# A common sum joins its last product in the PSUM bank: the down projection of a two-layer streaming encoder

## The chip, the cores and the metric

The kernel runs on one core of a Trainium2 chip. The metric is device time in microseconds (us) of one execution; smaller is better. TensorE does the matrix products, VectorE (DVE), ScalarE (ACT) and GpSimd (POOL) the element work, and SyncE (SP) issues most transfers.

## The reference

Two layers of a transformer encoder with D_MODEL = 1024 are computed for 1152 tokens (1024 of a prompt and 8 x 16 of running streams). Each layer does attention, then a SwiGLU feed-forward with D_FF = 2816:

```python
def swiglu(h, w_in, w_out):
    gate, up = jnp.split(h @ w_in, 2, axis=-1)
    return (jax.nn.silu(gate) * up) @ w_out

for layer in range(DEPTH):
    ...
    xp = xp + swiglu(rmsnorm(xp, norm_ffn[layer]), w_ffn_in[layer], w_ffn_out[layer])
    xs = xs + swiglu(rmsnorm(xs, norm_ffn[layer]), w_ffn_in[layer], w_ffn_out[layer])
y_prompt = rmsnorm(xp, norm_final)
```

The change touches the last product of this, `(...) @ w_out` added to x: the down projection, once in each layer. All in float32.

## The kernel before

**Numbers in two parts.** A float32 operand is split into a rounded part (`hi`, by ACT, L284) and the rest (`lo`, by `split2`, L285, on POOL or DVE). A product is three matmuls, hi by hi, hi by lo and lo by hi (`passes`, L191 to L193), into one PSUM bank. All have 128 rows and 288 columns (`QW`).

**The down projection** (`down`, called once per layer) adds W_out times the hidden values to x. Of the 22 blocks of 128 hidden rows four are done plainly: two ahead (`firsts`) and two at the end (`finals`), by `step`, L1271. The other 18 are nine pairs in three groups of three pairs (`GROUPS`), and each pair is a Strassen-Winograd scheme of seven products on half-size blocks, in the order b11, t1, t2, t3, t4, b21, b22 (`ORDER`). The sums on the side of the hidden values come from DRAM (`hds`), those on the weights' side are made here (`prep_a`). `product` runs one of the seven for one of 8 output tiles (4 values of j by 2 of q): 3 pairs by 3 matmuls into one bank, then DVE adds the bank to x or to the common sum (L1331). With x seen as four blocks, x11 = `xq(q, j)`, x12 = `xq(2 + q, j)`, x21 = `xq(q, j + 4)`, x22 = `xq(2 + q, j + 4)`: b11 goes to x11 and to the common sum u (`us`, 8 tiles), t1 to x12 and x22, t2 to u, t3 (P7 in the title of the change) to x21 and x22, t4 to x21, b21 to x11, b22 to x12.

**The common sum.** u is complete when t2 of the last group has been added. It belongs to x12, x21 and x22. `combine` (L1334) adds it to them on POOL (L1335), three adds for each of the 8 (j, q), 24 in a layer; they are merged into the work of t3, t4 and b21 of the last group.

**What sets the order.** `merge` deals the preparation of a product (`prep_b`: load and split three pages of hidden sums, POOL; `prep_a`: weight sums and splits, POOL, but for b22 on DVE) between the tiles of the product before. A scheduler then orders the instructions of each engine by its own simulated times; each engine runs its list strictly in that order. PSUM banks come from `ps_any`, which takes the tags m, s, t, s in turn, with 2, 3 and 2 banks. A tile with tag s therefore needs the bank of the tile six before it, and that bank's DVE add done.

**Names in the rows.** `ps` is a bank, `wh` and `wr` weights or their parts, `sd` the weight sum of a pair, `wd` raw weights, `pg` a page (hidden values, their parts, or u), `x` the result, `hd` and `hds` the hidden values in DRAM.

Of the kernel before, what the change touches and what calls it, by code (L numbers as in the profile page):

```python
# [15 lines left out]
ALU = mybir.AluOpType  # L16
# [5 lines left out]
KT = D // P  # L22
# [25 lines left out]
GROUPS = ((1, 2, 3), (4, 5, 6), (7, 8, 9))  # L48
DOWN = ("b11", "t1", "t2", "t3", "t4", "b21", "b22")
ORDER = DOWN  # L50
# [10 lines left out]
def model(ctx: ExitStack, tc: tile.TileContext, I, O):  # L61
    nc = tc.nc
    V, A, G, S, E = nc.vector, nc.scalar, nc.gpsimd, nc.sync, nc.tensor
# [4 lines left out]
    def sb(name, side="left"):  # L68
        return tc.tile_pool(name=name, bufs=1, side=side, reuse_waits="tile")
# [10 lines left out]
    ident = cons.tile([P, P], F32, name="ident")  # L80
# [106 lines left out]
    def passes(out, wts, acts, first=True, last=True, seen=False):  # L187

        n = len(wts)
        for i, ((wh_, wl_), (xh_, xl_)) in enumerate(zip(wts, acts)):  # L190
            E.matmul(out, wh_, xh_, start=first and i == 0, stop=False, skip_group_check=seen)  # L191
            E.matmul(out, wh_, xl_, start=False, stop=False, skip_group_check=seen)  # L192
            E.matmul(out, wl_, xh_, start=False, stop=last and i == n - 1, skip_group_check=seen)  # L193
# [358 lines left out]
    stores, finals = [], []  # L552
# [45 lines left out]
    def merge(*lists):  # L598

        tot = [max(sum(c for c, _ in l), 1) for l in lists]  # L600
        pos, done, out = [0] * len(lists), [0.0] * len(lists), []
        while any(p < len(l) for p, l in zip(pos, lists)):
            i = min((i for i, l in enumerate(lists) if pos[i] < len(l)),
                    key=lambda i: (done[i] + lists[i][pos[i]][0] / 2) / tot[i])
            out.append(lists[i][pos[i]])
            done[i] += out[-1][0]
            pos[i] += 1
        return out
# [342 lines left out]
    def xq(q, k):  # L951

        return X[q // 2][k // 2][:, k % 2, q % 2 * QW:(q % 2 + 1) * QW]
# [14 lines left out]
    def page(n, shape=(4, QW), dt=F32R):  # L968
        return pages[(n >= 8) + (n >= 12) + (n >= 18)].tile([P, *shape], dt, name=nm("pg"), tag=f"g{n}", bufs=1)
# [275 lines left out]
    def down(layer, name, last):  # L1245

        wb = ExitStack()
        pb = wb.enter_context(sb(name + "wb"))
        src = I["w_ffn_out"][layer]
        hrs, bp, ap = [0], [0], [0]  # L1250

        def staged(src, shape):
            t = page(8 + hrs[0] % 4, shape, F32)
            hrs[0] += 1
            S.dma_start(t, src)
            return t


        def prep(f, ops, eng):
            w = weights(src[2 * PLAIN[f // 2] + f % 2], (KT, P), None, eng)  # L1260
            raw = staged(hd[f], (T,))
            hi, lo = (page(f % 2 + n, (T,)) for n in (0, 2))
            split2(hi, lo, raw, eng)
            ops.append((w, (hi, lo)))

        def step(ops, q, j, hook=None):
            o = ps_any()
            c0 = q * QW
            passes(o[:, :QW], [(w[0][:, j, :], w[1][:, j, :]) for w, _ in ops],
                   [(h[0][:, c0:c0 + QW], h[1][:, c0:c0 + QW]) for _, h in ops])  # L1270
            V.tensor_tensor(xq(q, j), xq(q, j), o[:, :QW], ALU.add)  # L1271
            if hook is not None:
                hook(q, j)


        us = [page(4 + q, (4, QW), F32) for q in range(2)]

        def group_load(st, r):

            for k, p in enumerate(st["pairs"]):  # L1280
                st["w", r, k] = t = pb.tile([P, D], F32, name=nm("wd"), tag="wd", bufs=9)
                S.dma_start(t, src[2 * p + r])

        def prep_a(st, n, k):
            f, f1 = st["w", 0, k], st["w", 1, k]
            a11, a12, a21, a22 = f[:, :512], f1[:, :512], f[:, 512:], f1[:, 512:]
            if n == "t1":
                st["s", k] = pb.tile([P, 512], F32, name=nm("sd"), tag="sd", bufs=3)
            z = st.get(("s", k))
            if n == "t1":  # L1290
                G.tensor_tensor(z, a21, a22, ALU.add)
            elif n == "t2":
                V.tensor_tensor(z, z, a11, ALU.subtract)
            elif n == "t3":
                G.tensor_tensor(a11, a11, a21, ALU.subtract)
            elif n == "b22":
                V.tensor_tensor(z, a12, z, ALU.subtract)
            raw = {"b11": a11, "t3": a11, "t4": a22, "b21": a12}.get(n, z)
            i = ap[0] % 3
            if i == 0:  # L1300
                ap[1:] = [wp.tile([P, 2, 4 * VW], F32R, name=nm("wh"), tag="wh", bufs=3)]
            if i < 2:
                hi, lo = (ap[1][:, z, 512 * i:512 * (i + 1)] for z in range(2))
            else:
                t = wp.tile([P, 4 * VW], F32R, name=nm("wr"), tag="wr", bufs=3)
                hi, lo = t[:, :512], t[:, 512:1024]
            ap[0] += 1
            split2(hi, lo, raw, G if n != "b22" else V)
            st[n, "a", k] = hi, lo

        def prep_b(st, n, k):
            raw = staged(hds[st["pairs"][k], DOWN.index(n)], (HALF,))
            t = page((6, 7, 12, 13, 14, 15, 16, 17)[bp[0] % 8], (2, HALF))
            bp[0] += 1
            split2(t[:, 0], t[:, 1], raw, G)
            st[n, "b", k] = t

        def product(st, n, j, q):
            o = ps_any()[:, :QW]
            c = slice(q * QW, (q + 1) * QW)  # L1320
            ks = range(len(st["pairs"]))
            passes(o, [tuple(z[:, j * P:(j + 1) * P] for z in st[n, "a", k]) for k in ks],
                   [(st[n, "b", k][:, 0, c], st[n, "b", k][:, 1, c]) for k in ks])
            u = us[q][:, j]
            x11, x12, x21, x22 = xq(q, j), xq(2 + q, j), xq(q, j + 4), xq(2 + q, j + 4)
            for z in {"b11": (x11, u), "t1": (x12, x22), "t2": (u,), "t3": (x21, x22), "t4": (x21,),
                      "b21": (x11,), "b22": (x12,)}[n]:
                if n == "b11" and z is u and st["first"]:
                    A.copy(u, o)
                else:  # L1330
                    V.tensor_tensor(z, z, o, ALU.add)  # L1331

        def combine(j, q):
            for z in (xq(2 + q, j), xq(q, j + 4), xq(2 + q, j + 4)):  # L1334
                G.tensor_tensor(z, z, us[q][:, j], ALU.add)  # L1335

        firsts, finals = [], []
        run([(1, lambda f=f: prep(f, firsts, V)) for f in range(2)])
        run(x_load(lambda h, i: xd[h, :, 2 * i:2 * i + 2]))
        work, preps = [], []  # L1340
        for i, g in enumerate(GROUPS):
            st = {"pairs": g, "first": i == 0}
            for n in ORDER:
                l = [(1, lambda st=st, r=r: group_load(st, r)) for r in range(2)] if n == ORDER[0] else []
                for k in range(len(g)):
                    l.append((1, lambda st=st, n=n, k=k: prep_b(st, n, k)))
                    l.append((1, lambda st=st, n=n, k=k: prep_a(st, n, k)))
                preps.append(l)
                w = [(1, lambda st=st, n=n, j=j, q=q: product(st, n, j, q)) for j in range(4) for q in range(2)]
                if i == len(GROUPS) - 1 and n in ORDER[3:6]:  # L1350
                    z = ORDER.index(n) - 3
                    w = merge(w, [(1, lambda j=j, q=q: combine(j, q)) for j, q in
                                  [(j, q) for j in range(4) for q in range(2)][3 * z:3 * z + 3]])
                work.append(w)
        preps.append([(1, lambda f=f: prep(f, finals, V)) for f in (2, 3)])
        run(merge([(1, lambda q=q, j=j: step(firsts, q, j)) for q in range(4) for j in range(KT)], preps[0]))
        for w, l in zip(work, preps[1:]):
            run(merge(w, l))
        wb.close()
        pgs[2].close()  # L1360
        pgs[1].close()
        last(lambda q, hook: [(1100, lambda j=j: step(finals, q, j, hook)) for j in range(KT)])
        pgs[0].close()

    def block_tail(li, o_scr, w_src, last, beside=None):
# [126 lines left out]
    with sb("px0", "right") as px:  # L1492
        table(AF.Abs_reciprocal_sqrt)
        first, pre, post = [], [], []
        for ci, (c0, c1) in enumerate(FIRST):
# [7 lines left out]
            st = {}  # L1503
# [73 lines left out]
    with sb("pin1", "right") as pin:  # L1577
        first = [proj_k(I["w_kc"], act, pin, O["c_kt"], kh["c"], kl["c"], ksm["c"], lambda: ps_any("sts")),
                 proj_vt(I["w_vc"], act, pin, O["c_vt"], vs["c"], vsm["c"])]
# [184 lines left out]
```

## Time and profile before

| | |
|---|---|
| median of 3 runs | 2807.08 us (2805.0 to 2810.45) |
| the profiled execution, its own time | 2804.28 us |
| its span (first to last instruction) | 2802.5 us |
| PE busy | 2633.9 us, 94% of the span |
| DVE busy | 1694.0 us, 60% |
| POOL busy | 1247.3 us, 45% |
| ACT busy | 1141.5 us, 41% |
| mean granted TensorE clock, share of full speed | 0.966 |

Busy time is an average over stages with different limits, so the stage in question has to be read by itself. The down projection's groups and finals run from about 1327 to 1560 us in layer 0 and to about 2758 us in layer 1. A row of the timeline has the start, the length (both us), the engine, the line, the operation, output and inputs, the number of instructions merged into the row, and in brackets how long the engine was idle before and who ended that.

### The profile page before, as it was taken

Reading aid. Unit: us, or ns where it says so; the run is one execution under the profiler, and the core shown is the slowest. Engines: PE = TensorE matmul, PEld = TensorE weight load, DVE = VectorE, ACT = ScalarE, POOL = GpSimd, SP = SyncE. Lnnn points to the kernel's source line nnn. Section 1 sums busy time; section 2 is a strip of 40 time slices with the busy share of each in tenths; the row PEclk is TensorE's granted clock in tenths of the full one; section 3 lists DMA queues with packets and bytes.
Section 4 is the critical chain, followed back from the end, with each engine's and each line's share of the span. In section 5 each row is a group of like instructions: output and inputs, shape, how many; then the busy total and the mean of one; then the engine's idle time right before and its main releaser. Section 6 shows DMA issues by size and latency. Waiting matters only on the chain.

```text
span 2802.5 us, 52586 instructions
## 1 busy us (share of the span) xinstructions
PE 2633.9 (94%) x19742; PEld 2522.2 (90%) x19742; DVE 1694.0 (60%) x3583; ACT 1141.5 (41%) x2510; POOL 1247.3 (45%) x1152
## 2 busy tenths in 40 slices
PE   8999988998989999999998998879799999999987
PEld 7999966777989999999998998869799999999987
DVE  7110266766686565566677766855955556556677
ACT  5221366776342222323332566754422222224323
POOL 4212132233443444444996432233434444349993
PEclk8999998999999999999998999989899999999998
DMA  5546587885213232337432132332123223264322
GB/s 159 168 140 205 175 231 227 265 270 179 70 61 103 80 101 86 102 96 244 128 114 90 65 110 81 102 112 64 70 73 98 93 95 99 93 213 165 120 65 91
DMA packets 209840, 357.63 MB, mean 128 GB/s; under 512 B 27817, under 2 KB 134449, under 8 KB 207537
## 3 DMA queue, kind: packets, MB, share of 16 engines
q1 hardware_dynamic: 204976, 349.55, 40.1%
q10 hardware_dynamic: 4608, 4.72, 0.5%
q8 instruction: 155, 2.54, 0.4%
q14 instruction: 101, 0.82, 0.1%
HBM read 252.22 MB, written 101.95 MB: 126 GB/s over the span
## 4 chain that ended last, share of the span: by engine, by line
PE 68%; DVE 10%; DMA 8%; POOL 6%; issue 5%; ACT 2%; SPq 1%; DVEq 0%; ACTq 0%; POOLq 0%
PE ps L191 18%; PE ps L192 18%; PE ps L193 17%; POOL pg L285 2%; PE ps L544 2%; POOL wh L285 2%; PE ps L507 2%; DMA oraw<-od 1%; DVE hf L281 1%; PE ps L505 1%; PE ps L574 1%; DVE pg L285 1%; PE ps L397 1%; PE ps L398 1%; PE ps L396 1%
## 5 line engine op out<-in xcount | busy, mean ns | idle before, releaser
L191 PE MATMUL ps<-pg,wh 128*128 128x288 f32 x3200 | 952.2, 299 | 46.0 <-DVE x L1331 27.0
L192 PE MATMUL ps<-pg,wh 128*128 128x288 f32 x3200 | 952.3, 298 | 3.3 <-POOL pg L285 2.5
L193 PE MATMUL ps<-pg,wh 128*128 128x288 f32 x3200 | 937.4, 296 | 0.6 <-DVE wh L285 0.6
L191 PEld LDWEIGHTS ps<-pg,wh 128*128 128x128 f32 x3200 | 606.5, 190 | 51.4 <-DVE x L1331 27.5
L192 PEld LDWEIGHTS ps<-pg,wh 128*128 128x128 f32 x3200 | 608.5, 190 | 4.8 <-POOL pg L285 3.1
L193 PEld LDWEIGHTS ps<-pg,wh 128*128 128x128 f32 x3200 | 604.3, 190 | 1.2 <-DVE wh L285 0.8
L285 POOL TENSOR_TENSOR wh<-wr,wh 128x1024 fp32r<-128x1024 f32 (+1 forms) x96 | 232.6, 2426 | 349.6 <-ACT wh L284 340.0
L284 ACT CAST wh<-wr 128x1024 fp32r<-128x1024 f32 (+2 forms) x156 | 161.1, 1036 | 248.0 <-PE ps L193 217.9
L192 PE MATMUL ps<-hl,wh 128*128 128x288 f32 x832 | 248.2, 300 | 2.5 <-DVE hl L285 2.3
L191 PE MATMUL ps<-hh,wh 128*128 128x288 f32 x832 | 246.5, 302 | 4.2 <-ACT hh L284 3.1
L193 PE MATMUL ps<-hh,wh 128*128 128x288 f32 x832 | 245.5, 297 | 0.0
L285 POOL TENSOR_TENSOR pg<-pg,pg 128x576 fp32r<-128x576 f32 x126 | 194.8, 1560 | 26.2 <-ACT pg L284 26.2
L1331 DVE TENSOR_TENSOR x<-x,ps 128x288 f32<-128x288 f32 x384 | 156.5, 447 | 81.3 <-PE ps L193 81.1
L284 ACT CAST pg<-pg 128x576 fp32r<-128x576 f32 (+1 forms) x134 | 90.9, 702 | 270.6 <-PE ps L193 145.6
L285 POOL TENSOR_TENSOR wh<-x,wh 128x1024 fp32r<-128x1024 f32 x42 | 101.0, 2406 | 151.2 <-ACT wh L284 151.2
L191 PEld LDWEIGHTS ps<-hh,wh 128*128 128x128 f32 x832 | 156.9, 191 | 8.2 <-ACT hh L284 5.0
L192 PEld LDWEIGHTS ps<-hl,wh 128*128 128x128 f32 x832 | 158.8, 191 | 4.6 <-DVE hl L285 3.4
L193 PEld LDWEIGHTS ps<-hh,wh 128*128 128x128 f32 x832 | 158.6, 191 | 0.1
L285 POOL TENSOR_TENSOR x<-wr,x 128x512 fp32r<-128x512 f32 x44 | 58.5, 1330 | 213.3 <-ACT x L284 208.5
L1191 DVE TENSOR_TENSOR u<-p,ps 128x288 f32<-128x288 f32 x176 | 78.9, 448 | 111.9 <-PE ps L193 111.7
L549 DVE TENSOR_TENSOR pl<-ps,ph 128x512 fp32r<-128x512 f32 (+1 forms) x152 | 92.3, 611 | 34.5 <-ACT ph L548 33.9
L191 PE MATMUL ps<-x,wh 128*128 128x288 f32 x352 | 105.4, 299 | 5.7 <-DVE x L1195 5.7
(296 smaller groups left out, 6202.9 us busy)
## 6 DMA issues: line engine op xcount, KB each, us to landing
wr<-w_ffn_in SPq DMA_DIRECT2D x88, 512.0 KB
hds<-hd SPq DMA_DIRECT2D x252, 144.0 KB
pg<-hds SPq DMA_DIRECT2D x126, 288.0 KB
wd<-w_ffn_out SPq DMA_DIRECT2D x36, 512.0 KB
wr<-w_out SPq DMA_DIRECT2D x22, 512.0 KB
xd<-x SPq DMA_DIRECT2D x16, 576.0 KB
x<-xd SPq DMA_DIRECT2D x16, 576.0 KB
svt<-cache_a_v SPq DMA_DIRECT2D x8, 1024.0 KB
```

Of the source, the lines that this page charges most:

```text
L191: E.matmul(out, wh_, xh_, start=first and i == 0, stop=False, skip_group_check=seen)
L192: E.matmul(out, wh_, xl_, start=False, stop=False, skip_group_check=seen)
L193: E.matmul(out, wl_, xh_, start=False, stop=last and i == n - 1, skip_group_check=seen)
L281: V.scalar_tensor_tensor(out, src, gains[:, gi, k:k + 1], rs, ALU.mult, ALU.mult)
L284: A.copy(hi, src)
L285: eng.tensor_tensor(lo, src, hi, ALU.subtract)
L396: E.matmul(o[:, :width], xh_[:, k], wts[k][0], start=k == 0, stop=False)
L507: E.matmul(sp[:, :w], q2[:, qt], kl2[:, k0:k0 + w], start=False, stop=not dg)
L544: E.transpose(pt[:, col:col + P], tl[:, (kb - kb0) * P:(kb - kb0 + 1) * P], ident)
L549: V.tensor_tensor(fl, pt[:, lo_:hi_], fh, ALU.subtract)
L1191: V.tensor_tensor(st[n, q], st["p1", q], st["x", q][:, :QW], ALU.add)
L1331: V.tensor_tensor(z, z, o, ALU.add)
```

## The change

In the last group, product t3 does not close its bank after its nine matmuls: a tenth one, with the identity as the weights and u as the moving operand, in plain float32, adds u in the bank (L1328). DVE's adds of the bank to x21 and x22 then carry u along. `combine` keeps only the add to x12, 8 in a layer, and moves from the last group's products to the first quarter (q = 0) of the plain block `finals`, behind each of its 8 steps.

```diff
             ks = range(len(st["pairs"]))
+            u = us[q][:, j]
+            fold = n == "t3" and st["last"]
             passes(o, [tuple(z[:, j * P:(j + 1) * P] for z in st[n, "a", k]) for k in ks],
-                   [(st[n, "b", k][:, 0, c], st[n, "b", k][:, 1, c]) for k in ks])
-            u = us[q][:, j]
+                   [(st[n, "b", k][:, 0, c], st[n, "b", k][:, 1, c]) for k in ks], True, not fold)
+            if fold:
+
+                E.matmul(o, ident, u, start=False, stop=True)
...
         def combine(j, q):
-            for z in (xq(2 + q, j), xq(q, j + 4), xq(2 + q, j + 4)):
-                G.tensor_tensor(z, z, us[q][:, j], ALU.add)
+
+            z = xq(2 + q, j)
+            G.tensor_tensor(z, z, us[q][:, j], ALU.add)
...
-                if i == len(GROUPS) - 1 and n in ORDER[3:6]:
-                    z = ORDER.index(n) - 3
-                    w = merge(w, [(1, lambda j=j, q=q: combine(j, q)) for j, q in
-                                  [(j, q) for j in range(4) for q in range(2)][3 * z:3 * z + 3]])
...
-        last(lambda q, hook: [(1100, lambda j=j: step(finals, q, j, hook)) for j in range(KT)])
+
+        def final(q, j, hook):
+            step(finals, q, j, hook)
+            if q == 0:
+                combine(j % 4, j // 4)
+
+        last(lambda q, hook: [(1100, lambda j=j: final(q, j, hook)) for j in range(KT)])
```

How the instructions move, in layer 0 (layer 1 has the same). On **POOL**, in the last group, these rows stood behind the second weight split of t4 (x_2661 and x_2662 hold x12, x_2659 and x_2660 x21, x_2663 and x_2664 x22; pg_15581 and pg_15582 are u):

```order
L1335 TENSOR_TENSOR x_2662_15615<-x_2662_15615,pg_15582 128x288
L285 TENSOR_TENSOR pg_18070<-pg_18068,pg_18070 128x576
L285 TENSOR_TENSOR wh_18087<-wd_17473,wh_18087 128x512
L285 TENSOR_TENSOR wh_18087<-wd_17475,wh_18087 128x512
L1335 TENSOR_TENSOR x_2659_15609<-x_2659_15609,pg_15581 128x288
L1335 TENSOR_TENSOR x_2663_15617<-x_2663_15617,pg_15581 128x288
L285 TENSOR_TENSOR pg_18114<-pg_18112,pg_18114 128x576
L285 TENSOR_TENSOR wr_18163<-wd_17477,wr_18163 128x512
L1335 TENSOR_TENSOR x_2659_15609<-x_2659_15609,pg_15582 128x288
```

and now the same place reads so:

```order
L285 TENSOR_TENSOR pg_18069<-pg_18067,pg_18069 128x576
L285 TENSOR_TENSOR wh_18083<-wd_17473,wh_18083 128x512
L285 TENSOR_TENSOR wh_18083<-wd_17475,wh_18083 128x512
L285 TENSOR_TENSOR pg_18099<-pg_18097,pg_18099 128x576
L285 TENSOR_TENSOR wr_18153<-wd_17477,wr_18153 128x512
L285 TENSOR_TENSOR pg_18139<-pg_18137,pg_18139 128x576
L285 TENSOR_TENSOR pg_18180<-pg_18178,pg_18180 128x576
L285 TENSOR_TENSOR pg_18211<-pg_18209,pg_18211 128x576
L285 TENSOR_TENSOR pg_18252<-pg_18250,pg_18252 128x576
L1340 TENSOR_TENSOR x_2661_15613<-x_2661_15613,pg_15581 128x288
L1340 TENSOR_TENSOR x_2661_15613<-x_2661_15613,pg_15582 128x288
```

The adds have left their places between the splits; the eight that remain (L1340) stand together behind the last split for b22, and each reads an x12 to which DVE must first have added b22.

On **DVE**, behind the last adds of t3 (L1331 and, in the changed file, L1335 are the adds of a bank; the `wh` and `wr` rows of width 512 are b22's splits, those of width 1152 the splits of the finals' hidden values), before:

```order
L285 TENSOR_TENSOR wh_18208<-sd_17597,wh_18208 128x512
L285 TENSOR_TENSOR wh_18208<-sd_17643,wh_18208 128x512
L285 TENSOR_TENSOR wr_18283<-sd_17676,wr_18283 128x512
L1331 TENSOR_TENSOR x_2659_15609<-x_2659_15609,ps_18057 128x288
L1331 TENSOR_TENSOR x_2659_15609<-x_2659_15609,ps_18076 128x288
L1331 TENSOR_TENSOR x_2660_15611<-x_2660_15611,ps_18133 128x288
L1331 TENSOR_TENSOR x_2660_15611<-x_2660_15611,ps_18149 128x288
```

and now:

```order
L285 TENSOR_TENSOR wh_18195<-sd_17597,wh_18195 128x512
L1335 TENSOR_TENSOR x_2659_15609<-x_2659_15609,ps_18056 128x288
L285 TENSOR_TENSOR wh_18195<-sd_17643,wh_18195 128x512
L285 TENSOR_TENSOR wr_18267<-sd_17676,wr_18267 128x512
L1335 TENSOR_TENSOR x_2659_15609<-x_2659_15609,ps_18072 128x288
L1335 TENSOR_TENSOR x_2659_15609<-x_2659_15609,ps_18086 128x288
L1335 TENSOR_TENSOR x_2659_15609<-x_2659_15609,ps_18102 128x288
L285 TENSOR_TENSOR pg_18311<-pg_18308,pg_18310 128x1152
L1335 TENSOR_TENSOR x_2660_15611<-x_2660_15611,ps_18113 128x288
L285 TENSOR_TENSOR pg_18366<-pg_18363,pg_18365 128x1152
L1335 TENSOR_TENSOR x_2660_15611<-x_2660_15611,ps_18126 128x288
```

b22's splits keep their place ahead of t4's adds; the two splits of the finals' hidden values, which stood among and behind the adds of b21, now stand ahead of the fifth and the sixth add of t4. (On SP their two loads went ahead of the two weight loads of the finals, which stood ahead of each of them.)

## Rows read from the trace of the kernel before

**Rows 1.** What PE waited for, stretch 1470 to 1550 us (2680 to 2760 answers alike).

```profile
PE ps L191 <- DVE x L1331: 13.5, 1, 13.5
```

**Rows 2.** Timeline of PE around these two waits, layer 0, then layer 1.

```profile
1503.77 0.29 PE L191 MATMUL ps<-pg,wh 128*128 128x288 f32 x1
1504.83 0.29 PE L193 MATMUL ps<-pg,wr 128*128 128x288 f32 x1
1518.61 0.61 PE L191 MATMUL ps<-pg,wh 128*128 128x288 f32 x1 [13.48 <-DVE x L1331]
...
2710.88 0.30 PE L193 MATMUL ps<-pg,wr 128*128 128x288 f32 x1
2724.72 0.61 PE L191 MATMUL ps<-pg,wh 128*128 128x288 f32 x1 [13.55 <-DVE x L1331]
```

**Rows 3.** Timeline of DVE over the wait in layer 0, and the same operation in layer 1.

```profile
1499.67 17.32 DVE L285 TENSOR_TENSOR wh<-sd,wh 128x512 fp32r<-128x512 f32 x1 [0.85 <-ACT wh L284]
1516.91 0.68 DVE L285 TENSOR_TENSOR wh<-sd,wh 128x512 fp32r<-128x512 f32 x1
...
2705.71 17.39 DVE L285 TENSOR_TENSOR wh<-sd,wh 128x512 fp32r<-128x512 f32 x1 [0.82 <-ACT wh L284]
```

**Rows 4.** Timeline of POOL over the wait in layer 0.

```profile
1497.42 2.56 POOL L285 TENSOR_TENSOR wh<-wd,wh 128x512 fp32r<-128x512 f32 x2
1499.92 1.59 POOL L1335 TENSOR_TENSOR x<-x,pg 128x288 f32<-128x288 f32 x2
...
1504.06 6.07 POOL L1335 TENSOR_TENSOR x<-x,pg 128x288 f32<-128x288 f32 x8
1510.05 1.44 POOL L285 TENSOR_TENSOR pg<-pg,pg 128x576 fp32r<-128x576 f32 x1
...
1515.61 0.83 POOL L1335 TENSOR_TENSOR x<-x,pg 128x288 f32<-128x288 f32 x1
1519.36 0.80 POOL L1335 TENSOR_TENSOR x<-x,pg 128x288 f32<-128x288 f32 x1 [2.92 <-DVE x L1331]
```

**Rows 5.** Stretches in and behind the waits: length, busy (count) of PE, PEld, DVE, ACT, POOL; PEclk.

```profile
1499.92:1516.44 16.52, 5.21 (x40) 4.97 (x38) 16.52 (x1) 1.36 (x3) 16.52 (x19) 0.72 0.07 19
1518.61:1524.61 6.00, 6.00 (x25) 6.00 (x26) 2.67 (x7) 0.67 (x1) 3.52 (x4) 0.52 0.07 13
2724.72:2729.39 4.67, 4.67 (x19) 4.67 (x20) 1.50 (x4) 0.67 (x1) 2.18 (x3) 0.51 0.00 2
```

**Rows 6.** b22's splits in group one of layer 0, timeline of DVE and POOL.

```profile
1365.60 0.87 DVE L285 TENSOR_TENSOR wh<-sd,wh 128x512 fp32r<-128x512 f32 x1 [0.30 <-ACT wh L284]
1365.88 1.88 POOL L285 TENSOR_TENSOR pg<-pg,pg 128x576 fp32r<-128x576 f32 x1
1366.76 1.56 DVE L285 TENSOR_TENSOR wh<-sd,wh 128x512 fp32r<-128x512 f32 x1
```

**Rows 7.** A float32 matmul of the same shape between others, and one at low clock.

```profile
738.78 0.29 PE L193 MATMUL ps<-pg,wh 128*128 128x288 f32 x1
738.92 0.65 PE L211 MATMUL ps<-acc,ones 128*128 128x288 f32 x2
739.19 0.51 PE L191 MATMUL ps<-pg,wh 128*128 128x288 f32 x1
739.53 0.29 PE L192 MATMUL ps<-pg,wh 128*128 128x288 f32 x1
...
1999.98 1.33 PE L211 MATMUL ps<-acc,ones 128*128 128x288 f32 x2 [5.04 <-POOL acc L206]
```

**Rows 8.** A page cast of b21; then load, cast, split of the finals' hidden values.

```profile
1497.25 0.68 ACT L284 CAST pg<-pg 128x576 fp32r<-128x576 f32 x1 [6.13 <-PE ps L193]
...
1523.75 0.38 SPq L1255 DMA_DIRECT2D pg<-hd  x1
1528.73 1.16 ACT L284 CAST pg<-pg 128x1152 fp32r<-128x1152 f32 x1 [0.29 <-DMA pg<-hd]
1533.20 1.35 DVE L285 TENSOR_TENSOR pg<-pg,pg 128x1152 fp32r<-128x1152 f32 x1
```

More of the change, by code (lines that the diff above doesn't have):

```diff
@@ L1341, in down @@
         for i, g in enumerate(GROUPS):
-            st = {"pairs": g, "first": i == 0}
+            st = {"pairs": g, "first": i == 0, "last": i == len(GROUPS) - 1}
             for n in ORDER:
```

## The prediction

> **What bounds the kernel now.** I read the stage before the whole: the waits of PE in the down projection's last group, then PE's, DVE's and POOL's timelines over them. PE is the bound of this stage, and in the last group of each layer it waits just once, for 13.5 us, for a DVE add of L1331 [rows 1]. The timeline shows where: PE runs at a pitch of 0.1325 us a matmul (1503.77 to 1504.83 is eight pitches), stops behind the matmul that starts at 1504.83 and goes on at 1518.61 [rows 2]. That is 1518.61 - 1504.83 - 0.13 = 13.65 us; in layer 1, from 2710.88 to 2724.72, 13.71 us. I call the start of product t4 T. The matmul at 1503.77 opens a tile of t4, tiles are 9 x 0.1325 = 1.19 us apart and PE stops behind this one, the sixth, which is what the rotation of tags allows without an add; so T is 1497.8, and the stop comes at T + 7.2.
>
> Why is there no add? DVE's first split for b22 begins at 1499.67 and lasts 17.32 us, where the same operation next takes 0.68 us; in layer 1 it lasts 17.39 us [rows 3]. All adds of t4 stand behind it in DVE's list. Beside it POOL works without a gap from 1497.42 to 1515.61 + 0.83 = 1516.44: 18 instructions from 1499.92 on (19 counted with the one just ending [rows 5]), 13 adds of the common sum and five of its own splits, with eight adds in 6.07 us as the longest piece [rows 4]. POOL then has nothing to do until 1519.36, and the split is over at 1516.91, 0.5 us after POOL's last instruction. I read this as: DVE's split, with two inputs in SBUF, was held as long as POOL kept going, and what kept POOL going was the adds.
>
> After each stop PE runs at the lower clock for a while: 25 matmuls in 6.00 us at a granted 0.52, and 19 in 4.67 us at 0.51 [rows 5], that is the level of 1.2 GHz in place of 2.4. At the pitch of 0.1325 they would take 3.31 and 2.52 us, so the stops cost another 2.69 and 2.15 us. Together the two stops cost 13.65 + 2.69 + 13.71 + 2.15 = **32.2 us**.
>
> The Trainium skill, "SBUF — State Buffer", section "Who interferes with whom", says that a DVE instruction with two SBUF inputs and a GpSimd instruction that reads SBUF exclude each other, and that the second waits until the first has finished. The trace agrees that they exclude each other, but here DVE waited for 18 POOL instructions in a row, not for one.
>
> **The change, part by part.**
>
> *The float32 matmuls.* 8 in a layer, 16 in all, on the engine that bounds the stage, between product tiles that wait for nothing in t3. Price: in a running stream a float32 matmul of this shape (two records in the trace) moved the next matmuls from 738.92 and 739.05 to 739.19 and 739.53 [rows 7], 0.48 us later. 16 x 0.48 = **+7.7 us**. Bounds: nothing below that, since no wait is there to hide them; above, the 1.33 us of one that ran at low clock behind a wait [rows 7], 16 x 1.33 = 21.3 us. I take 0.48, since t3 runs in a full stream at the full clock. Their operand u was finished a whole product (9.5 us) earlier, so they add no wait.
>
> *The 32 POOL adds taken away.* 16 in a layer at 6.07 / 8 = 0.76 us [rows 4], 12.1 us of POOL's time in t3, t4 and b21. POOL's time counts only through the split that it holds. What is left beside b22's splits is POOL's own splits for the same products. Groups one and two had that already: there the first splits of b22 took 0.87 and 1.56 us beside POOL splits, one of which ran from 1365.88 [rows 6]. From above: if DVE were held until POOL is out of work, POOL has at the end of t3 three page splits that come free there, 3 x 1.44 = 4.3 us [rows 4]; the adds of t4 would come at about T + 6, still ahead of T + 7.2, where PE needs the first. So by both ends the stop goes: **-32.2 us**.
>
> *The 8 adds moved* (per layer). Each needs b22's add on DVE first, so none can run beside b22's splits, and the eight come at the pace of b22's tiles, 1.19 us, against 0.76 us for an add. Behind them on POOL stand a weight split of the next part and the squares of the finals; in front of the first reader, the third quarter of the finals, lie two quarters of 8 x 6 matmuls, 12.7 us. Cost zero; if that cover were gone, one add, 0.76 us a layer. In DVE's list no instruction with two SBUF inputs stands among b22's adds.
>
> *The finals' hidden values.* Their splits on DVE now stand ahead of the fifth and sixth add of t4, their loads ahead of the weights' loads on SP. A load takes 1528.73 - 1523.75 = 5.0 us to the cast, the cast 1.16, the split 1.35 us [rows 8]. The first needs a raw page that POOL frees with the second of the three page splits, the second one that it frees with the third. The pages' parts come free at T - 0.6 (the cast that PE released at 1497.25, 0.68 us [rows 8]), so the first load leaves at about T - 0.6 + 0.7 + 2 x 1.44 = T + 3.0, the second 1.4 us later. So the second split would be over at about T + 4.4 + 5.0 + 1.2 + 1.4 = T + 12.0, and the seventh add at T + 12.8. PE needs that add for tile 13, at T + 12 x 1.19 = T + 14.3. Spare: 1.5 us. Cost zero, but this is what is late next: each us beyond the spare is a us of PE in each layer, plus up to 2.7 us for the clock.
>
> Sum, against the profiled execution's own 2804.28 us (span 2802.5): 2804.28 - 32.2 + 7.7 = 2779.8. That execution is 2.8 us under the median of the runs shown, which would give 2782.6. I say **2781**.
>
> **The rivals.**
>
> *Part of the stop stays.* The finals' hidden values land 3 us later than the spare allows, or DVE is held somewhat longer than reckoned. For it: three loads of pages go together there, and the spare is an estimate out of six numbers. Against it: the 5.0 us is itself from a load that shared the engines with another. 2 x (3 + 2.7) = 11.4 us more: 2791.
>
> *POOL stays as late as now, and the adds of t4 wait behind the hidden values: slower.* In the kernel before, the three page splits in question run from 1510.05 to the last before 1515.61, that is T + 12.3 to T + 17.9 [rows 4]. With the same lateness the second load would go out at T + 17.9, its split end at T + 25.5 and the seventh add at T + 26.3, 12 us after PE needs it. With the clock that is 14.7 us, and with the matmuls 18.5 us against 16.1 us won in a layer: 2809. It decides from the point where the second load leaves later than about T + 15.5. Against it: POOL's lateness was the adds, 12.1 us in each layer, and they go.
>
> *The split is not held by POOL's adds.* DVE's split waits for one POOL instruction at most, 1.44 us [rows 4], and the rest of its 17.3 us has a source that the change doesn't touch, such as its own inputs; then both stops stay and the matmuls are added: 2804.28 + 7.7 = 2812. For it: in [rows 6] a split got in between two POOL instructions. Against it: it ended 0.5 us behind POOL's last instruction, and its twin behind it took 0.68 us. That the loser waits for one instruction is the rule of the Trainium skill, "SBUF — State Buffer", "Who interferes with whom".
>
> **How the numbers follow.** Forecast 0.75, part of the stop 0.13, POOL late 0.05, not POOL 0.05; 0.02 for what I don't see. A run tells a difference of over 0.2%, 5.6 us, from no change. The forecast and the partial stop are both faster, so faster 0.89, and the two others are slower or at the edge: slower 0.08, same 0.03. The forecast's own range is 2775 to 2786 (2779.8 and 2782.6, and some us for the scheduler's other shifts). The range runs from 2774 to 2794, up to the partial stop and to the upper price of the matmuls (2779.8 + 13.6 = 2793.4).
>
> **What would show it.** In the changed profile: no wait of PE in the last group longer than 1 us; b22's first split in DVE's timeline under 4 us; no granted clock of 0.5 there; 32 records of L1328 with the next tile 0.48 us later each; POOL with gaps before t4 ends. A wait of PE ended by L1335 in b21, with the split of width 1152 just before, is the partial stop; the old wait at the old length behind a 17 us split would make me wrong.

## The result, and the profile after

In the first comparison the changed kernel took 2777.32 us (median of 4 runs, 2776.07 to 2780.07) against 2806.04 us of the kernel before on the same chip: ratio 0.9896, 95% interval 0.9881 to 0.9911, faster. Two more comparisons, made beside experiments below, gave 2785.80 us (6 runs, ratio 0.9930, 0.9915 to 0.9945) and 2782.38 us (6 runs, 0.9910, 0.9892 to 0.9928). All three intervals lie more than 0.5% below 1. The profiled execution of the first took 2780.07 us (span 2778.3, mean clock 0.969), against 2804.28 us before.

The whole time wanders by several us in parts that the change doesn't touch, so I also measure the groups of the down projection by themselves. In each layer they run from DVE's first add of a product (L1331, in the changed file L1335) to its first add of L1271 for the finals. Timeline of DVE, kernel before:

```profile
1327.51 0.46 DVE L1331 TENSOR_TENSOR x<-x,ps 128x288 f32<-128x288 f32 x1 [0.73 <-PE ps L193]
...
1543.75 0.45 DVE L1271 TENSOR_TENSOR x<-x,ps 128x288 f32<-128x288 f32 x1 [0.34 <-PE ps L193]
...
2533.59 0.46 DVE L1331 TENSOR_TENSOR x<-x,ps 128x288 f32<-128x288 f32 x1 [0.74 <-PE ps L193]
...
2749.36 0.46 DVE L1271 TENSOR_TENSOR x<-x,ps 128x288 f32<-128x288 f32 x1 [0.34 <-PE ps L193]
```

The same rows of the changed kernel:

```profile
1329.81 0.45 DVE L1335 TENSOR_TENSOR x<-x,ps 128x288 f32<-128x288 f32 x1 [0.74 <-PE ps L193]
...
1533.53 0.46 DVE L1271 TENSOR_TENSOR x<-x,ps 128x288 f32<-128x288 f32 x1 [0.34 <-PE ps L193]
...
2521.46 0.46 DVE L1335 TENSOR_TENSOR x<-x,ps 128x288 f32<-128x288 f32 x1 [0.74 <-PE ps L193]
...
2725.22 0.45 DVE L1271 TENSOR_TENSOR x<-x,ps 128x288 f32<-128x288 f32 x1 [0.34 <-PE ps L193]
```

Before, the groups take 216.24 and 215.77 us, after 203.72 and 203.76: 24.53 us less for both layers, where the forecast has 32.2 - 7.7 = 24.5. The expectations below count from the first plain part on. That adds 29.1 to 32.0 us a layer, in which PE waits for other adds of DVE, up to 2.2 us at a time; from the groups' first add on, the three profiles of the changed kernel agree to 0.01 us a layer. From the finals' first add of layer 1 to the end of the span, 53.1 us pass in both (2802.5 - 2749.36, 2778.3 - 2725.22): nothing was given back there.

The list of PE's waits has no row left where [rows 1] stood, nor in layer 1. Two stretches of the last group, around the place of the stop, show PE busy throughout at a granted clock of 1.00, where [rows 5] had stops and 0.5 behind them (columns as there):

```profile
1485.00:1500.00 15.00, 15.00 (x108) 14.47 (x107) 6.64 (x16) 3.39 (x6) 13.78 (x11) 1.00 0.43 119
1500.00:1515.00 15.00, 15.00 (x111) 14.68 (x110) 11.59 (x19) 6.36 (x9) 6.45 (x4) 1.00 0.29 87
```

PE's timeline around the last float32 matmul of t3 gives its price and the start of t4, T = 1503.72:

```profile
1503.32 0.29 PE L193 MATMUL ps<-pg,wr 128*128 128x288 f32 x1
1503.45 0.65 PE L1328 MATMUL ps<-pg,ident 128*128 128x288 f32 x2
1503.72 0.51 PE L191 MATMUL ps<-pg,wh 128*128 128x288 f32 x1
1504.07 0.29 PE L192 MATMUL ps<-pg,wh 128*128 128x288 f32 x1
```

From 1503.32 to 1504.07 two pitches (0.265 us) have become 0.75: 0.485 us for a matmul, where [rows 7] said 0.48. DVE's splits, against [rows 3]: b22's three, then the finals' two hidden values (width 1152), and the first split in layer 1:

```profile
1504.87 0.77 DVE L285 TENSOR_TENSOR wh<-sd,wh 128x512 fp32r<-128x512 f32 x1
...
1505.93 1.55 DVE L285 TENSOR_TENSOR wh<-sd,wh 128x512 fp32r<-128x512 f32 x1
1507.41 1.92 DVE L285 TENSOR_TENSOR wr<-sd,wr 128x512 fp32r<-128x512 f32 x1
...
1510.34 1.35 DVE L285 TENSOR_TENSOR pg<-pg,pg 128x1152 fp32r<-128x1152 f32 x1
...
1512.97 1.36 DVE L285 TENSOR_TENSOR pg<-pg,pg 128x1152 fp32r<-128x1152 f32 x1 [0.92 <-ACT pg L284]
...
2696.54 0.76 DVE L285 TENSOR_TENSOR wh<-sd,wh 128x512 fp32r<-128x512 f32 x1
```

POOL over the same stretch, against [rows 4]:

```profile
1503.66 5.12 POOL L285 TENSOR_TENSOR pg<-pg,pg 128x576 fp32r<-128x576 f32 x3 [4.87 <-ACT pg L284]
1513.67 1.95 POOL L285 TENSOR_TENSOR pg<-pg,pg 128x576 fp32r<-128x576 f32 x1 [4.90 <-ACT pg L284]
1525.84 2.33 POOL L1340 TENSOR_TENSOR x<-x,pg 128x288 f32<-128x288 f32 x3 [10.21 <-DVE x L1335]
...
1533.27 0.81 POOL L1340 TENSOR_TENSOR x<-x,pg 128x288 f32<-128x288 f32 x1 [0.38 <-DVE x L1335]
1534.04 2.40 POOL L285 TENSOR_TENSOR wh<-wr,wh 128x1024 fp32r<-128x1024 f32 x1
```

POOL has paused for 4.87 us when t4 begins. Beside b22's splits it has three page splits and then 4.90 us of nothing. The splits take turns with them, and the longest lasts 1.92 us in place of 17.32. The moved adds come at the pace of b22's tiles and end 0.55 us behind the finals' first add.

### The profile page after: what moved, and what is told of

It reads as the page before. It is cut to its first block, busy times and chain, and to the rows that moved or that the text cites. A ratio compares the mean times of both kernels' runs of the same rounds, so it can differ in the third digit from the quotient of the medians.

```text
span 2778.3 us, 52629 instructions
## 1 busy us (share of the span) xinstructions
PE 2639.6 (95%) x19774; PEld 2525.9 (91%) x19774; DVE 1661.7 (60%) x3583; ACT 1139.7 (41%) x2510; POOL 1229.6 (44%) x1120
## 4 chain that ended last, share of the span: by engine, by line
PE 77%; DVE 9%; DMA 7%; issue 2%; ACT 2%; POOL 1%; SPq 1%; DVEq 0%; ACTq 0%; POOLq 0%
PE ps L191 21%; PE ps L192 21%; PE ps L193 20%; PE ps L544 2%; PE ps L507 2%; DVE hf L281 1%; PE ps L505 1%; PE ps L397 1%; PE ps L396 1%; PE ps L398 1%; DMA oraw<-od 1%; PE ps L574 1%; DVE pg L285 1%; PE ps L575 1%; DVE h L281 1%
## 5 line engine op out<-in xcount | busy, mean ns | idle before, releaser
L1335 DVE TENSOR_TENSOR x<-x,ps 128x288 f32<-128x288 f32 x384 | 158.1, 447 | 89.3 <-PE ps L193 74.8
```

## The experiments

All groups in one table: their time per layer (layer 0, layer 1), b22's first split on DVE, PE's longest wait for an add in t4 to b22, and the median with its ratio to the kernel before.

| kernel | groups, us | first split, us | wait, us | median, us | ratio |
|---|---|---|---|---|---|
| before | 216.24, 215.77 | 17.32, 17.39 | 13.5, 13.5 | 2806.04 | 1 |
| the change | 203.72, 203.76 | 0.77, 0.76 | none | 2777.32 | 0.9896 (0.9881 to 0.9911) |
| the change, 2nd | 203.73, 203.75 | 0.77, 0.76 | none | 2785.80 | 0.9930 (0.9915 to 0.9945) |
| the change, 3rd | 203.72, 203.76 | 0.77, 0.76 | none | 2782.38 | 0.9910 (0.9892 to 0.9928) |
| no matmuls | 199.90, 199.89 | 0.87, 0.87 | none | 2774.74 | 0.9889 (0.9870 to 0.9908) |
| adds back | 207.88, 206.48 | 8.43, 8.41 | 2.5, 2.5 | 2786.82 | 0.9933 (0.9914 to 0.9952) |
| x12 moved only | 208.69, 209.26 | 11.93, 11.88 | 6.3, 6.3 | 2790.66 | 0.9930 (0.9908 to 0.9951) |
| adds late | 202.72, 200.35 | 8.17, 0.96 | 2.6, none | 2779.71 | 0.9910 (0.9875 to 0.9946) |
| memset each | 203.73, 203.76 | 0.77, 0.76 | none | 2780.44 | 0.9914 (0.9896 to 0.9933) |
| copy each | 203.74, 203.84 | 0.84, 0.85 | none | 2780.99 | 0.9917 (0.9897 to 0.9938) |
| adds placed | 199.90, 199.89 | 0.87, 0.87 | none | 2786.14 | 0.9936 (0.9920 to 0.9952) |
| copy twice | 210.11, 210.49 | 6.42, 6.42 | 2.1, 2.5 | 2798.23, one run | |
| memset thrice | 203.72, 203.76 | 0.68, 0.68 | none | 2785.26, one run | |
| adds spread | 200.25, 199.89 | 0.87, 0.87 | none | 2772.71 | 0.9884 (0.9867 to 0.9900) |

**Without the matmuls.** Edit to the changed kernel:

```
-                   [...], True, not fold)
-            if fold:
-                E.matmul(o, ident, u, start=False, stop=True)
+                   [...])
```

> The changed kernel without its 16 float32 matmuls; the sums x21 and x22 lack the common sum, all else stays. Theory A (the matmuls cost their 0.48 us each in a full stream and nothing else): 2777.3 - 7.7 = 2769.6 us, no wait of PE in the last group, the tiles of t3 again 1.19 us apart. Rival (the slack of t3 is used elsewhere: without them t4 starts 3.85 us earlier in each layer against the loads of the finals' hidden values, whose spare was reckoned as 1.5 us): a wait of PE in b21 or the finals gives part of it back, 2772 to 2777. Rival (they cost more than in the stream, up to 1.33 us each): 2756.

Timeline of DVE:

```profile
1324.22 0.45 DVE L1332 TENSOR_TENSOR x<-x,ps 128x288 f32<-128x288 f32 x1 [0.73 <-PE ps L193]
...
1524.12 0.46 DVE L1271 TENSOR_TENSOR x<-x,ps 128x288 f32<-128x288 f32 x1 [0.34 <-PE ps L193]
...
2517.86 0.46 DVE L1332 TENSOR_TENSOR x<-x,ps 128x288 f32<-128x288 f32 x1 [0.74 <-PE ps L193]
...
2717.75 0.45 DVE L1271 TENSOR_TENSOR x<-x,ps 128x288 f32<-128x288 f32 x1 [0.34 <-PE ps L193]
```

The groups of both layers take 399.79 us, and 407.48 us in each of the three profiles of the changed kernel. So the 16 matmuls cost 7.7 us, 0.48 us each: theory A, and neither rival. The medians of the whole don't show it: this one lies in the range of the first rival, and the three of the changed kernel lie 2.6 to 11.1 us above it; but PE has no wait in the last group, which that rival needs. And 432.01 - 399.79 = 32.2 us is what the stops cost, without the matmuls.

**The adds put back.** The changed kernel, and beside its matmuls the 16 adds on x21 and x22 where they were:

```
+        def both(j, q):
+            for z in (xq(q, j + 4), xq(2 + q, j + 4)):
+                G.tensor_tensor(z, z, us[q][:, j], ALU.add)
...
+                if i == len(GROUPS) - 1 and n in ORDER[3:6]:
+                    z = ORDER.index(n) - 3
+                    w = merge(w, [(1, lambda j=j, q=q: both(j, q)) ...[3 * z:3 * z + 3]])
```

> The changed kernel, with the 16 POOL adds of a layer put back where they stood, beside the matmuls (so x21 and x22 get the common sum twice); x12 stays in the finals. Only POOL's work beside b22's splits is changed. Theory A (POOL's unbroken run of adds and splits holds DVE's first b22 split): the split is held again, somewhat shorter than 17.3 us, since 16 adds in place of 24 stand in the run (some 9 in place of 13 beside the split, 4 x 0.76 = 3 us less), so about 14 us; PE stops about 10 us per layer in t4 and runs slow for 2 us after it: 2777.3 + 2 x 12 = 2801, between 2790 and 2810. Rival (it was the order of other work, or the eight x12 adds, that held it; the matmuls or the moved step cured it): no stop, 2777 to 2780. Rival (DVE loses one POOL instruction at a time): a split of 2 to 3 us, no stop, 2777 to 2780.

The hold is back in both layers, with the stop. Timeline of DVE, then of POOL, layer 0:

```profile
1499.76 8.43 DVE L285 TENSOR_TENSOR wh<-sd,wh 128x512 fp32r<-128x512 f32 x1
```

```profile
1495.10 7.66 POOL L1344 TENSOR_TENSOR x<-x,pg 128x288 f32<-128x288 f32 x10
1502.73 2.80 POOL L285 TENSOR_TENSOR pg<-pg,pg 128x576 fp32r<-128x576 f32 x2
1505.49 0.80 POOL L1344 TENSOR_TENSOR x<-x,pg 128x288 f32<-128x288 f32 x1
1506.25 1.39 POOL L285 TENSOR_TENSOR pg<-pg,pg 128x576 fp32r<-128x576 f32 x1
1511.66 1.58 POOL L1344 TENSOR_TENSOR x<-x,pg 128x288 f32<-128x288 f32 x2 [4.02 <-DVE x L1335]
```

The split ends at 1508.19, 0.55 us behind POOL's last instruction before its pause (1507.64). No moved step and no x12 add is needed: POOL's adds alone bring the hold. Nor is the order on DVE the cure: in the changed kernel t4's first add already stands behind the first of b22's splits, as the list of the change shows, and here it stands there too (it begins at 1508.11). The size that I expected (14 us, 2801, at least 2790) was too large: 2786.82. I had taken the hold before and subtracted four adds; but with eight adds fewer ahead of it, and with a t3 that the matmuls make 3.85 us longer, POOL is also earlier, so more of its run was over when the split came.

**x12 moved, nothing folded.** The same adds, without the matmuls.

> The kernel before with x12's eight adds a layer moved to the finals, as the change has them, and nothing folded: 16 adds stay on POOL in t3, t4 and b21, no float32 matmul. Theory A: the hold of about 14 us as with the adds put back, without the 7.7 us of matmuls: 2801 - 7.7 = 2793, between 2782 and 2802; the stop begins 7.2 us behind the start of t4. Rival (the x12 adds were the ones that held the split): 2770, no stop. Rival (taking eight adds away shortens nothing, since POOL's end is set by its own splits' sources): the stops stay whole, 2804.

Held in both layers, for 11.9 us; PE waits 6.3 us twice and then runs low (granted 0.60 and 0.50 in the 6 us behind). In layer 0 the split runs from 1502.73 to 1514.66, and POOL's last instruction before a pause ends at 1512.67 + 1.44 = 1514.11:

```profile
1512.67 1.44 POOL L285 TENSOR_TENSOR pg<-pg,pg 128x576 fp32r<-128x576 f32 x1
1518.13 1.55 POOL L1341 TENSOR_TENSOR x<-x,pg 128x288 f32<-128x288 f32 x2 [4.02 <-DVE x L1332]
```

Again the split ends 0.55 us behind it. In all these pauses POOL waits for an add of DVE (the brackets here, above and in [rows 4]), and that add stands behind the held split: POOL went on until it could do no more without DVE. The groups take 417.95 us, 18.2 more than without the 16 adds a layer. So moving x12 gives 432.01 - 417.95 = 14.1 us of the change's gain, and taking the 16 adds away the other 18.2, for 7.7 of matmuls.

**Adds late.** No matmuls; x21's adds written among b22's tiles, x12's and x22's into the first two quarters of the finals.

```
...
-            if q == 0:
-                combine(j % 4, j // 4)
+            if q < 2:
+                combine(j % 4, j // 4, xq(2 + j // 4, j % 4 + 4 * q))
```

> A kernel that is meant to beat both: no float32 matmul, all 24 adds of a layer stay on POOL but none beside b22's splits: x21's eight go among the tiles of b22, x12's eight into the first quarter of the finals, x22's eight into the second. Theory A (the adds cost only through the DVE split that they hold): 2777.3 - 7.7 = 2769.6, no PE wait in t4. Rival (adds on POOL hold whatever DVE split is beside them): the finals' weight splits, some 14 and 20 us behind the start of t4, are held by the adds among b22's tiles and the finals start late: 2775 to 2790, with a wait of PE at the finals' start. Rival (the squares of the finals stand behind the adds on POOL): the norm of the first quarter is late, with a wait of PE of some us behind the finals: 2773 to 2780.

The place in the text didn't hold them: the scheduler drew x22's eight adds forward, into t3 and t4, so that theory A's kernel wasn't tried. What came of it is the most telling profile of all, since the two layers differ. DVE's first split, layers 0 and 1, and POOL around each:

```profile
1499.11 8.17 DVE L285 TENSOR_TENSOR wh<-sd,wh 128x512 fp32r<-128x512 f32 x1 [0.30 <-ACT wh L284]
...
2693.80 0.96 DVE L285 TENSOR_TENSOR wh<-sd,wh 128x512 fp32r<-128x512 f32 x1 [0.30 <-ACT wh L284]
```

```profile
1497.23 4.63 POOL L1334 TENSOR_TENSOR x<-x,pg 128x288 f32<-128x288 f32 x6
1501.82 2.80 POOL L285 TENSOR_TENSOR pg<-pg,pg 128x576 fp32r<-128x576 f32 x2
1504.59 0.79 POOL L1334 TENSOR_TENSOR x<-x,pg 128x288 f32<-128x288 f32 x1
1505.35 1.39 POOL L285 TENSOR_TENSOR pg<-pg,pg 128x576 fp32r<-128x576 f32 x1
...
2691.82 6.03 POOL L1334 TENSOR_TENSOR x<-x,pg 128x288 f32<-128x288 f32 x6
```

In layer 0 the split comes 1.88 us into the six adds and waits through the rest of them and four more instructions. In layer 1 it comes 1.98 us into the same six adds, and it and its two twins get in between them (0.96, 0.93, 0.93 us; the six adds take 6.03 us in place of 4.63). So a run of POOL's can hold the split, but needn't. The four runs of this kernel spread from 2770.91 to 2793.75 us.

**One memset, one copy for an add.** In the kernel with the adds put back, `G.memset(z, 0.0)` or `G.tensor_copy(z, us[q][:, j])` in place of the add.

> The changed kernel with 16 POOL memsets of a layer where the 16 adds stood (each sets the 128x288 tile of x21 or x22 to zero, so these sums are lost), in place of the adds put back in the earlier run, whose splits were held 8.4 us. POOL is as unbroken as there, if with shorter instructions, but these read nothing from SBUF. Theory A1 (what excludes DVE's two-input split is POOL reading SBUF): the split is not held beyond 3 us, no stop, 2777 to 2780. Rival A2 (any unbroken run of POOL's instructions holds it, whether they read or not): held 4 to 8 us, a stop of 0 to 2.5 us a layer, 2780 to 2787.

> The same with 16 POOL copies of the common sum's tile over x21 and x22 (one SBUF input in place of two). Theory A1 (reading SBUF excludes): the split is held as with the adds, 5 to 8.4 us, and PE stops up to 2.5 us a layer: 2780 to 2787. Rival A3 (only a two-input POOL instruction excludes a two-input DVE one): no hold beyond 3 us, 2777 to 2780.

No hold in either, but neither says which operations hold. The memset takes 0.31 us and the copy 0.38, so their runs ended (at 1500.99 and 1494.77, layer 0) before b22's first split began (1503.85, 1496.85). They show only that no hold comes once POOL's long run is over; with the four instructions that POOL had left beside the splits, these took turns.

**Two copies, three memsets.** The same with `for _ in range(2)` and `range(3)` around them.

> The changed kernel with two POOL copies of the common sum's tile where each of the 16 adds stood (the sums x21 and x22 are overwritten). With one copy each, POOL's copies had ended before b22's first split began, so that run did not try what it was meant to; two take 0.75 us, as one add does, so that the split should begin amid them. Theory A1 (POOL reading SBUF back to back excludes the split, whatever the operation): held as with the adds, 5 to 8.4 us. Rival A3 (only a two-input POOL instruction excludes a two-input DVE one): the split takes below 3 us although copies run back to back beside it.

> The same with three POOL memsets in place of each add (some 0.9 us), which read nothing from SBUF. Theory A1 (what excludes is reading): the split takes below 2 us while memsets run back to back beside it. Rival A2 (any unbroken run of POOL's excludes): held 5 us or more, until POOL pauses.

Copies, which read one input, hold it. Timeline of DVE, then of POOL:

```profile
1502.96 6.42 DVE L285 TENSOR_TENSOR wh<-sd,wh 128x512 fp32r<-128x512 f32 x1
```

```profile
1502.70 2.90 POOL L285 TENSOR_TENSOR pg<-pg,pg 128x576 fp32r<-128x576 f32 x2
1505.46 0.88 POOL L1345 COPY x<-pg 128x288 f32<-128x288 f32 x2
1506.22 1.51 POOL L285 TENSOR_TENSOR pg<-pg,pg 128x576 fp32r<-128x576 f32 x1
1507.58 1.26 POOL L1345 COPY x<-pg 128x288 f32<-128x288 f32 x3
1511.38 1.17 POOL L1345 COPY x<-pg 128x288 f32<-128x288 f32 x3 [2.53 <-DVE x L1335]
```

It waits through eight instructions, splits and copies, and ends at 1509.38, 0.54 us behind the last (1508.84). Layer 1 has the same 6.42 us. Memsets, which read nothing from SBUF, don't hold it:

```profile
1503.82 0.68 DVE L285 TENSOR_TENSOR wh<-sd,wh 128x512 fp32r<-128x512 f32 x1
1504.79 0.68 DVE L285 TENSOR_TENSOR wh<-sd,wh 128x512 fp32r<-128x512 f32 x1
1505.39 1.92 DVE L285 TENSOR_TENSOR wr<-sd,wr 128x512 fp32r<-128x512 f32 x1
```

```profile
1498.19 7.07 POOL L1345 MEMSET x<- 128x288 f32 x25
1505.23 1.54 POOL L285 TENSOR_TENSOR pg<-pg,pg 128x576 fp32r<-128x576 f32 x1
1506.70 0.61 POOL L1345 MEMSET x<- 128x288 f32 x2
```

Two splits begin inside the run of 25 memsets and take 0.68 us, as beside an idle POOL. The third meets a page split of POOL, waits for that one, and runs beside the two memsets behind it. So it is POOL's reading of SBUF that excludes, in adds, splits and copies alike. The Trainium skill, "SBUF — State Buffer", section "Who interferes with whom", says just this (two SBUF inputs on DVE contend with a GpSimd instruction that reads SBUF, not with one that only writes it), and these two profiles agree.

**Adds placed.** No matmuls; all 24 adds on POOL, chained by order edges behind its last page split for b22.

```
...
+        def combine(j, q, z):
+            with tc.issue_after(mark[-1].ins):
+                i = G.tensor_tensor(z, z, us[q][:, j], ALU.add)
+            mark.append(i)
...
```

> A kernel meant to beat both: no float32 matmul; all 24 adds of a layer on POOL, chained behind its last page split for b22 (x21's eight first, then x12's eight as b22's tiles come, then x22's eight), so that none can stand beside b22's splits, which the run with late adds showed the scheduler does by itself. Theory A: no stop, no hold of b22's splits, as the kernel without the matmuls: 2774 us; the first weight split of the finals may be held up to 4 us by x21's eight adds, inside the 7 us that PE's banks allow. Rival (POOL's 24 adds now end behind the start of the finals, and the squares of the first quarter come late): a wait of PE behind the finals of some us, 2776 to 2785. Rival (the hold of a finals' split lasts as long as the whole run of adds): PE stops in b21 or b22, 2780 to 2795.

> The changed kernel itself, beside the placed one on the same chip, so that the price of the matmuls (7.7 us by theory A, 2.6 us by the medians so far, 7.5 us by the two profiled runs) has an interval. Theory A: 2777, no stop; the difference to the placed kernel 3 to 7 us.

The groups are as short as without matmuls, 7.7 us below the changed kernel beside it, but the whole is the same (2786.14 against 2785.80): the first rival, 1 us above its range. POOL, layer 1:

```profile
2725.33 9.98 POOL L1339 TENSOR_TENSOR x<-x,pg 128x288 f32<-128x288 f32 x13 [1.59 <-DVE x L1333]
2735.25 1.71 POOL L239 TENSOR_TENSOR sq<-sq,sq 128x288 f32<-128x288 f32 x2
```

13 adds stand ahead of the finals' squares, which begin 8.5 us behind the finals' first add (2726.78), in the changed kernel 1.9 us (2727.08 against 2725.22). From that first add to the end of the span it is now 57.3 us in place of 53.1. These adds cost 4.2 us in the last layer; the rest of the 7.7 went behind layer 0's finals, where PE's waits in the 91 us from the first add on come to 8.1 us, against 4.3 to 4.8 in the three profiles of the changed kernel.

**Adds spread.** As placed, but x22's eight adds on DVE, one behind each add of b22's tiles, and x12's in the order of the tiles:

```
...
+                    i = V.tensor_tensor(z, z, o, ALU.add)
+            if n == "b22" and st["last"]:
+                with tc.issue_after(i.ins):
+                    V.tensor_tensor(x22, x22, u, ALU.add)
...
-                combine(j % 4, j // 4)
+                combine(j // 2, j % 2, xq(2 + j % 2, j // 2))
```

> A kernel meant to beat both: no float32 matmul; x21's eight adds of a layer on POOL behind its last page split for b22; x22's eight on DVE, one behind each add of b22's tiles, where DVE has 0.7 us free in each 1.19 us; x12's eight on POOL, each behind its tile of b22. Theory A: the down projection (first add of the first part to first add of the finals) takes 230.4 us in each layer as without the matmuls, against 234.3 of the changed kernel, and POOL is done 1.3 us after the finals begin, as in the changed kernel, so that nothing is given back there: 7.7 us below the changed kernel on the same chip. Rival (x21's adds hold the finals' first weight split, or DVE's and POOL's two-input adds exclude each other in b22): PE waits in b21 or b22, 230.4 becomes 235 or more, and nothing is won. Rival (POOL ends later and the finals' norm waits, as in the placed kernel, 4 us in a layer): the same time as the changed kernel.

> The changed kernel itself, beside the one with the adds spread, on the same chip. Theory A: 7.7 us above the spread one; down projection 234.3 us a layer; rival: the same time as it.

2772.71 us (4 runs, 2770.45 to 2779.23) against 2782.38 (6 runs, 2774.64 to 2788.68) of the changed kernel on the same chip. The intervals of the two ratios, each to the kernel before, overlap a little (0.9867 to 0.9900, 0.9892 to 0.9928), but the profiles say the same without that noise: the groups of both layers 400.14 us against 407.48. That is 7.3 us less where 7.7 were expected, and from the finals' first add to the end 53.35 against 53.1. This kernel beats both. POOL, layer 0, in b21 and b22:

```profile
1508.93 7.14 POOL L1342 TENSOR_TENSOR x<-x,pg 128x288 f32<-128x288 f32 x8
1519.63 7.85 POOL L1342 TENSOR_TENSOR x<-x,pg 128x288 f32<-128x288 f32 x8 [3.56 <-DVE x L1333]
```

In its DVE timeline the eight adds on x22 take about 0.70 us beside POOL's (0.45 for the first), and the finals' first weight split 1.91 us beside x21's adds: it got in between them, though after the runs above it could have been held there too.

## Why the prediction was right

**What bounds.** I said that DVE's split was held as long as POOL kept going, and that the adds kept POOL going. Shown: with the adds back the hold is back in both layers (8.4 us), with only x12 moved it stays (11.9 us), and each of these ends 0.55 us behind POOL's last instruction, as the one before did (I had 0.5 us, from the start of the next row; 1499.67 + 17.32 is 1516.99). The rival that the split waits for one POOL instruction at most is out: it waited through eight copies and splits.

**The stops, -32.2 us.** Without matmuls the groups are 32.2 us shorter than before. The term is right, and the sum has the clock's part (4.84 us) in it.

**The matmuls, +7.7 us.** 7.7 us by the groups, 0.485 us each by the row. They were paid in full, as a wait-free stage has it.

**From above.** I reckoned that three page splits would be POOL's only work there, 4.3 us, with t4's adds at T + 6 at the latest. It was these three, from T on (5.12 us, stretched by DVE's turns between them), and the third split of b22 ended at 1509.33, T + 5.6.

**The moved adds, cost zero.** They came at the pace of the tiles, and the time from the finals' first add to the end is 53.1 us in both. The cover is shorter than the 12.7 us that I gave it: in the placed kernel POOL was done with its adds 8.0 us later, and 4.2 us were lost.

**The hidden values, spare 1.5 us.** The second split was over at 1514.33, T + 10.6; I had T + 12.0. The partial stop didn't come, nor did the rival in which POOL stays late.

**The number.** 2804.28 - 32.2 + 7.7 = 2779.8 against 2780.07 of the profiled execution. In the groups that isn't luck: 24.53 us gained where 24.5 were forecast. For the whole it is: the rest of the span took 2370.5 us before and 2370.8 after, but 2376.5 and 2376.7 in the two other profiles of the changed kernel. The three medians, 2777.32, 2785.80 and 2782.38, lie around the forecast of 2781 and inside the range.

## What to carry to other kernels

A DVE instruction with two SBUF inputs that stands ahead of PE's evacuations should not be due while POOL has a backlog: look in the profile for one that lasts many times its twin's time and ends just behind POOL's last instruction before a pause. Then cut POOL's run at that place. It need not be cut by giving work to PE: the adds spread over POOL and DVE, behind the critical splits, were cheaper than float32 matmuls in a full stream. A gain inside a stage is best measured between two fixed rows of the trace between which no wait of another stage falls, and where the scheduler reorders, the place of an add in the text is no place in the queue; an order edge is.

## What the runs showed of the hardware that I had not expected

A hold that outlasts instructions: DVE waited through 18 POOL instructions before the change, and through eight when most of them were copies with one input. The Trainium skill, "SBUF — State Buffer", section "Summary: rules for kernel authors", has the second one wait until the first instruction has finished; by these runs it may go on waiting through all that POOL has queued.

But it isn't always so. In the changed kernel three page splits of POOL took turns with DVE's; in layer 1 of the kernel with late adds DVE got in between adds that held it in layer 0, having come at nearly the same point (1.98 and 1.88 us into them). What decides at POOL's change of instruction, these runs don't tell, and I leave it open.
